# A hybrid attention / state-space / delta-rule layer: convolution and gate-row DMAs moved from SyncE's queue to GpSimd's

## The chip, the core and the metric

The kernel runs on one core of a Trainium2 chip. The metric is the time of one execution on the device in microseconds (us). The core has TensorE (PE in the profile, with its weight loads as PEld), VectorE (DVE), ScalarE (ACT), GpSimd (POOL) and SyncE (SP). Each engine works through its own list of instructions in order. SP computes nothing here: its list is a list of DMA issues. A DMA issue that has to wait for a buffer or for another transfer holds up everything behind it in the list of the same engine.

## The reference

One layer on 256 tokens of width 4096. The input is RMS-normalised and multiplied by one wide matrix of 14392 columns. Those columns feed three groups of heads: a forgetting-attention group, a Mamba-2 group (SSD) and a gated DeltaNet group. Then a product with `w_out` and the residual. The parts that the change touches are the causal depthwise convolution over four tokens, which the DeltaNet q, k, v and the SSD x, B, C pass, and the cumulative gates ("rows" of decays) that each group needs on all partitions.

```
h    = rms_norm(x, norm_w)
proj = einsum('bsd,de->bse', h, w_in)            # 14392 columns, split among the groups
xbc  = silu(causal_depthwise_conv(ssd_xbc, ssd_conv_w) + ssd_conv_b)
qkv  = silu(causal_depthwise_conv(gdn_qkv, gdn_conv_w))
y    = ssd_scan(xs, dt, A, B, C)                 # decays exp(cumsum) between tokens
o    = gated_delta_rule(gq, gk, gv, g, beta)     # chunked solve, decays exp(cumsum)
o_f  = fox_attention(q, k, v, log_f)             # softmax with cumulated forget gates
out  = x + einsum('bse,ed->bsd', concat(o_f, y, o), w_out)
```

## The kernel before

The projection is cut into 28 panels of 512 columns (`UNITS`), and `w_out` into 8 more. A panel has 32 steps of 128 input rows. In each step a 128x512 piece of float32 weight is split into a high part `wh` (ScalarE, L203) and a low part `wl` (VectorE, L204). Six matmuls of 128x128 by 128x512 follow: for each of two blocks of tokens one with `wh` and the high part of x (L214), one with `wh` and the low part (L215), and one with `wl` (L216). There are 1152 such steps and 6912 such matmuls. They are the bulk of the program, and everything else is laid between them. The gate columns have a small product of their own at the start.

Weights come in pieces of two steps (512 KB, tile `wr`, four buffers) issued on SP by `panel` (L226) and, for the first two panels, by `first_panels` (L280). `wh` and `wl` have five buffers each, so ScalarE and VectorE can run at most five steps ahead of TensorE.

At the end of a panel ScalarE copies the two results out of PSUM into a tile `raw_...` (L1002, three buffers) and starts that unit's own work: a Python generator whose pieces are put between the steps by `drive()`, one piece per step; `yield 6` skips six steps. There are two lists of generators, `prep` (convolution and the like, one unit after another) and `core` (the heads themselves).

For a unit with a convolution, `conv_unit` stores the raw tile into a DRAM buffer `past` (L454), which has three zero rows in front, and reads it back shifted by one, two and three tokens (`shift`, L467). The four rows of filter weights are read as broadcasts over the partitions (`tap`, L458). VectorE multiplies and adds (L471, L476, L477, L485). There are 14 such units: gq, gk, gv for three groups, sB, sC, and sx for three thirds. `shift` tiles have two buffers, so the third shifted load waits until the first one is used up; `tap` tiles have three.

`gate_rows` (L423) reads rows of cumulated gates from a small DRAM tensor `gsum` as broadcasts (`dmat`, `e0`, `em`), 26 times; `gates` writes it once (L415). `clear_past` (L446) writes the zero rows.

All of these DMAs are issued on SP, between the loads of the weights. GpSimd has 73 instructions in the profile: a few elementwise products per head (`ktail` L571, `dmat` L600, `ds` L601, `tt` L639, `res` L664, `xd` L798 and so on).

The order on each engine is not the order of the text alone. The program is put in order by a list scheduler of the tile framework, which keeps a model of when each engine and queue is free; `pin` keeps the marked instructions in the order of the text among themselves. So a DMA that is put on another engine also changes where its neighbours stand.

Of the kernel before, what the change touches and what calls it, by code (L numbers as in the profile page):

```python
# [19 lines left out]
P = 128  # L20
D = 4096
T = 256
# [11 lines left out]
NSP = NDT + NGA + NFF  # L34
# [20 lines left out]
CONV = {}  # L55
# [3 lines left out]
TAPS = 4  # L59
# [32 lines left out]
def tile_hybrid(ctx: ExitStack, tc: tile.TileContext, x, xT, w, wo, prm, cst, lev, cvw, out):  # L92
    nc = tc.nc
# [12 lines left out]
    def r4(shape, dt=F32, name="r4", tag="acc"):  # L106
        return hp.tile(shape, dt, tag=tag, name=name, bufs=BUFS[tag])

    def t2(shape, dt=F32, name="t2", tag="t2"):
        return hp.tile(shape, dt, tag=tag, name=name, bufs=BUFS[tag])  # L110
# [7 lines left out]
    def bank(name="bank"):  # L118
        return ph.tile([P, 512], F32, tag="bank", name=name)
# [7 lines left out]
    def mid(ap, n):  # L127
        return ap.unsqueeze(1).broadcast_to([P, n, ap.shape[1]])


    pin = tc.keep_in_program_order
# [217 lines left out]
    def gates():  # L349
        gr = raw["gates"]  # L350
        pre = t2([P, 2, NSP], name="pre")
        nc.vector.tensor_tensor(out=pre, in0=gr[:, :, 0:NSP], in1=mid(prm_s[:, C_BIAS:C_BIAS + NSP], 2), op=ALU.add)
        f0 = NDT + NGA
        nc.vector.tensor_scalar_mul(pre[:, :, f0:NSP], pre[:, :, f0:NSP], -1.0)
        pf = pre.rearrange("p a b -> p (a b)")
        n = 2 * NSP
        ab = t2([P, n], name="g_ab")
        nc.vector.scalar_tensor_tensor(out=ab, in0=pf, scalar=-1.0, in1=pf, op0=ALU.mult, op1=ALU.max)
        e = t2([P, n], name="g_e")
        nc.scalar.activation(e, ab, AF.Exp, scale=-1.0)  # L360
        be = cp.tile([P, 2, NBE], F32, name="be")
        nc.scalar.activation(be, gr[:, :, NSP:NG], AF.Exp, scale=-1.0)
        ea = t2([P, NSP], name="ea")
        nc.vector.memset(ea[:, f0:NSP], -1.0)
        nc.scalar.activation(ea[:, 0:f0], prm_s[:, C_ALOG:C_ALOG + f0], AF.Exp)
        nc.vector.tensor_scalar_mul(ea[:, 0:f0], ea[:, 0:f0], -1.0)
        yield 2

        u = t2([P, n], name="g_u")
        nc.vector.tensor_scalar_add(u, e, 1.0)  # L370
        res = t2([P, n], name="g_r")
        nc.vector.scalar_tensor_tensor(out=res, in0=u, scalar=-1.0, in1=e, op0=ALU.add, op1=ALU.subtract)
        ru = t2([P, n], name="g_ru")
        nc.vector.reciprocal(ru, u)
        nc.vector.tensor_tensor(out=res, in0=res, in1=ru, op=ALU.mult)
        lu = t2([P, n], name="g_lu")
        nc.scalar.activation(lu, u, AF.Ln)
        yield 2
        nc.vector.tensor_tensor(out=lu, in0=lu, in1=res, op=ALU.subtract)
        spl = cp.tile([P, 2, NSP], F32, name="spl")  # L380
        nc.vector.scalar_tensor_tensor(out=spl.rearrange("p a b -> p (a b)"), in0=pf, scalar=0.0, in1=lu,
                                       op0=ALU.max, op1=ALU.add)
        ga = cp.tile([P, 2, NSP], F32, name="ga")
        nc.vector.tensor_tensor(out=ga, in0=spl, in1=mid(ea, 2), op=ALU.mult)
        yield

        nc.vector.tensor_scalar_add(be, be, 1.0)
        nc.vector.reciprocal(be, be)
        nbe = cp.tile([P, 2, NBE], F32, name="nbe")
        nc.vector.tensor_scalar_mul(nbe, be, -1.0)  # L390

        yield 2
        ps = bank("gps")
        nc.tensor.matmul(ps[:, 0:f0], U, ga[:, 1, 0:f0], start=True, stop=True)
        nc.tensor.matmul(ps[:, f0:2 * f0], SL, ga[:, 0, 0:f0], start=True, stop=True)
        dec = cp.tile([P, 2, f0], F32, name="dec")
        nc.scalar.activation(dec.rearrange("p a b -> p (a b)"), ps[:, 0:2 * f0], AF.Exp)


        yield  # L400
        ps = bank("csps")
        for tb, m in ((0, SL), (1, U)):
            o = tb * NSP
            nc.tensor.matmul(ps[:, o:o + f0], st["mid_u"], ga[:, tb, 0:f0], start=True, stop=True)
            nc.tensor.matmul(ps[:, o + f0:o + NSP], m, ga[:, tb, f0:NSP], start=True, stop=True)
        cs = cp.tile([P, 2, NSP], F32, name="csum")
        nc.vector.tensor_copy(cs.rearrange("p a b -> p (a b)"), ps[:, 0:2 * NSP])
        nc.vector.tensor_scalar_mul(cs[:, 1, f0:NSP], cs[:, 1, f0:NSP], -1.0)
        yield
        ps = bank("csrow")  # L410
        for tb in range(2):
            nc.tensor.transpose(ps[0:NSP, tb * P:tb * P + P], cs[:, tb, :], ident)
        rows = t2([P, 2, P], name="csrows")
        nc.scalar.copy(rows[0:NSP, :, :], ps[0:NSP, 0:2 * P].rearrange("p (a b) -> p a b", a=2))
        nc.sync.dma_start(out=gsum.rearrange("t h l -> h t l"), in_=rows[0:NSP, :, :])  # L415
        st.update(spl=spl, cs=cs, be=be, nbe=nbe, gam=dec[:, 0, :], tail=dec[:, 1, :])

    gsum = dp.tile([2, NSP, P], F32, name="gsum")

    def gate_rows(tb, c0, n, name, tag="t2", into=None):  # L420

        t = t2([P, n, P], name=name, tag=tag) if into is None else into
        pin(nc.sync.dma_start(out=t.rearrange("p a b -> p (a b)"),  # L423
                              in_=gsum[tb:tb + 1, c0:c0 + n, :].rearrange("o h l -> o (h l)").broadcast_to([P, n * P])))
        return t

    def decay(t, tb, c0, n):
# [11 lines left out]
    past = dp.tile([len(CONV), TAPS - 1 + T, 512], F32, name="past")  # L439

    def clear_past(after):
        z = t2([P, 512], name="zrows")
        nc.vector.tensor_copy(z[:, 0:1], after)
        nc.vector.memset(z, 0.0)
        for r in range(TAPS - 1):
            nc.sync.dma_start(out=past[:, r, :], in_=z[0:len(CONV), :])  # L446

    def conv_unit(name, dst=None, bias=False):


        src = raw.pop(name)
        i = list(CONV).index(name)
        yield
        pin(nc.sync.dma_start(out=past[i, TAPS - 1:TAPS - 1 + T, :].rearrange("(b p) c -> p b c", b=2), in_=src))  # L454

        def taps(r):
            t = t2([P, 512], name="tap", tag="tap")
            pin(nc.sync.dma_start(out=t, in_=cvw[i, r:r + 1, :].broadcast_to([P, 512])))  # L458
            return mid(t, 2)

        tap = [taps(r) for r in range(TAPS - 1, 0, -1)]
        yield 6

        def shifted(j):
            sh = r4([P, 2, 512], name="shift")
            r = TAPS - 1 - j
            pin(nc.sync.dma_start(out=sh, in_=past[i, r:r + T, :].rearrange("(b p) c -> p b c", b=2)))  # L467
            return sh

        got = [shifted(j) for j in (1, 2)]  # L470
        pin(nc.vector.tensor_tensor(out=src, in0=src, in1=tap[0], op=ALU.mult))  # L471
        yield
        tap.append(taps(0))
        yield 5
        for j in range(1, TAPS):
            pin(nc.vector.tensor_tensor(out=got[j - 1], in0=got[j - 1], in1=tap[j], op=ALU.mult))  # L476
            pin(nc.vector.tensor_tensor(out=src, in0=src, in1=got[j - 1], op=ALU.add))  # L477
            yield 1
            if j == 1:
                got.append(shifted(3))  # L480
                if bias:
                    tap.append(taps(TAPS))
            yield 1 if j == 1 else 4 if j == 2 else 1
        if bias:
            nc.vector.tensor_tensor(out=src, in0=src, in1=tap[TAPS], op=ALU.add)  # L485
            yield
        nc.scalar.activation(src if dst is None else dst, src, AF.Silu)  # L487
        yield
        return src
# [96 lines left out]
    def gdn_solve(g):  # L586

        qk, m32, m16 = [], [], []
        dr = [gate_rows(tb, NDT + HG * g, HG, "dmat") for tb in range(2)]
        yield 6  # L590
        for tb in range(2):
# [198 lines left out]
    def ssd_group(g):  # L790
        hh = slice(6 * g, 6 * g + 6)
        y_off = None
        for tb in range(2):
            xd = t2([P, 6, 64], name="xd", tag="qk")
            for u, a, n, o in pieces(g):
# [3 lines left out]
                                        op=ALU.mult)  # L799
            m = []  # L800
            dr = [gate_rows(tb, 6 * g + 3 * i, 3, "dmat") for i in range(2)]
            yield 6
            for i in range(2):
# [179 lines left out]
    def fox_out(g, z):  # L983
        yield from gated_norm(fx[f"ot{g}"], fx[f"c{g}"], z)
        yield from to_mix(fx[f"ot{g}"], 24 + 4 * g, C_FO)

    HEAD = {"ga": lambda i: gates(), "gq": gdn_q, "gk": gdn_k, "gv": gdn_v, "gz": gdn_z, "sB": ssd_b, "sC": ssd_c,
            "sx": ssd_x, "sz": ssd_z, "fq": fox_q, "fk": fox_k, "fv": fox_v, "fz": fox_z}

# [39 lines left out]
    for i in range(8):  # L1029
        cs = slice(i * 512, (i + 1) * 512)  # L1030
        ps = panel(wo[i].rearrange("p (j n) -> p j n", n=512), mix_split)
        for tb in range(2):
# [3 lines left out]
            n = 2 if i == 7 and tb == 1 else 1  # L1036
            for q in range(n):
# [3 lines left out]
                                                        in_=xr[:, qs])  # L1041
# [51 lines left out]
```

## Time and profile before

| | |
|---|---|
| median of 3 executions | 1717.98 us (1716.26 to 1718.16) |
| the profiled execution | 1718.33 us |
| its span, first to last instruction | 1716.5 us |
| PE busy | 1709.2 us (100%) |
| PEld busy | 1410.8 us (82%) |
| DVE busy | 1173.9 us (68%) |
| ACT busy | 930.1 us (54%) |
| POOL busy | 97.3 us (6%) |
| DMA moved | 368.87 MB, mean 215 GB/s |

Times in the views count from the first instruction of the span. A matmul's busy time is longer than the distance from its start to the next one's start, since they are pipelined; so 100% busy does not say that TensorE could not be faster, but a gap in it is a gap. Issuing instructions of SP are not counted as busy.

### The profile page before, as it was taken

The numbers are of one execution on the slowest core, as the hardware profiler recorded it, in microseconds if no ns is written. First come the engines' busy times: TensorE is split into PE (matmuls) and PEld (weight loads), VectorE is DVE, ScalarE is ACT, GpSimd is POOL, SyncE is SP. The second block draws the span as 40 slices with busy tenths as digits, with TensorE's granted clock in tenths as the row PEclk, the third lists the DMA queues.
The fourth block names the chain that finished last, engine by engine and source line by source line (L and its number), as shares of the span: only waits on it lengthen the run. The fifth ranks groups of instructions, "written<-read, shape, count | busy, mean of one in ns | idle before, by whom it ended". The sixth has DMA issues, their size and how long they took to land.

```text
span 1716.5 us, 24082 instructions
## 1 busy us (share of the span) xinstructions
PE 1709.2 (100%) x8165; PEld 1410.8 (82%) x8165; DVE 1173.9 (68%) x2121; ACT 930.1 (54%) x1611; POOL 97.3 (6%) x73
## 2 busy tenths in 40 slices
PE   9999999999999999999999999999999999999999
PEld 7888888888888788888888888888888888888887
DVE  7767777878776976869876765555656665555554
ACT  6665555455445544545555665556555754444443
POOL 0000030002000120001221100000000000000000
PEclk9999999999999999999999999999999999999999
DMA  8778777665766757758886666665666577777774
GB/s 288 232 240 272 257 244 228 221 202 164 248 208 205 244 172 225 246 172 295 261 257 196 184 184 186 193 196 172 185 194 192 178 236 217 218 218 215 208 208 136
DMA packets 119508, 368.87 MB, mean 215 GB/s; under 512 B 12629, under 2 KB 16045, under 8 KB 119383
## 3 DMA queue, kind: packets, MB, share of 16 engines
q1 hardware_dynamic: 114055, 358.15, 67.3%
q10 hardware_dynamic: 5328, 9.17, 1.5%
q8 instruction: 64, 1.05, 0.2%
q14 instruction: 61, 0.50, 0.1%
HBM read 355.61 MB, written 11.67 MB: 214 GB/s over the span
## 4 chain that ended last, share of the span: by engine, by line
PE 99%; DVE 0%; ACT 0%; issue 0%; DVEq 0%; ACTq 0%
PE proj L216 31%; PE proj L214 30%; PE proj L215 30%; PE kkps L610 1%; PE yp L818 1%; PE zps L583 0%; PE yps L583 0%; PE zqs L583 0%; PE gproj L243 0%; PE mps L508 0%; PE cor L583 0%; PE o L583 0%; PE vn L583 0%; PE atps L583 0%; PE warmps L154 0%; PE fps L900 0%
## 5 line engine op out<-in xcount | busy, mean ns | idle before, releaser
L204 DVE TENSOR_TENSOR wl<-wr,wh 128x512 fp32r<-128x512 f32 x1152 | 804.2, 711 | 480.6 <-ACT wh L203 418.2
L203 ACT CAST wh<-wr 128x512 fp32r<-128x512 f32 x1152 | 707.8, 621 | 713.1 <-PE proj L215 335.2
L214 PE MATMUL proj<-wh,xhl 128*128 128x512 f32 x1792 | 706.8, 395 | 2.1 <-ACT raw_gz L1002 1.9
L215 PE MATMUL proj<-wh,xhl 128*128 128x512 f32 x1792 | 701.2, 391 | 0.0
L216 PE MATMUL proj<-wl,xhl 128*128 128x512 f32 x1792 | 682.7, 395 | 0.0
L214 PEld LDWEIGHTS proj<-wh,xhl 128*128 128x128 f32 x1792 | 337.1, 188 | 72.2 <-ACT raw_gz L1002 2.3
L215 PEld LDWEIGHTS proj<-wh,xhl 128*128 128x128 f32 x1792 | 337.0, 188 | 69.1
L216 PEld LDWEIGHTS proj<-wl,xhl 128*128 128x128 f32 x1792 | 335.2, 188 | 68.6 <-DVE wl L204 0.2
L215 PE MATMUL proj<-wh,mhl 128*128 128x512 f32 x512 | 199.2, 389 | 0.0
L214 PE MATMUL proj<-wh,mhl 128*128 128x512 f32 x512 | 199.1, 390 | 0.0
L216 PE MATMUL proj<-wl,mhl 128*128 128x512 f32 x512 | 195.2, 390 | 0.0
L215 PEld LDWEIGHTS proj<-wh,mhl 128*128 128x128 f32 x512 | 96.1, 188 | 20.1
L214 PEld LDWEIGHTS proj<-wh,mhl 128*128 128x128 f32 x512 | 96.1, 188 | 19.9
L216 PEld LDWEIGHTS proj<-wl,mhl 128*128 128x128 f32 x512 | 96.1, 188 | 19.9
L476 DVE TENSOR_TENSOR shift<-shift,tap 128x1024 f32<-128x1024 f32 x42 | 52.5, 1250 | 8.3 <-DMA shift<-past 8.3
L655 DVE TENSOR_TENSOR tn<-tn,zps 128x512 f16<-128x512 f16 (+1 forms) x36 | 24.5, 681 | 3.7 <-PE zps L583 3.7
L656 DVE TENSOR_TENSOR tt<-tt,zqs 128x512 f16<-128x512 f16 (+1 forms) x36 | 24.4, 679 | 0.0
L664 POOL TENSOR_TENSOR res<-cst_s,tn 128x512 f32<-128x512 f32 x6 | 7.8, 1304 | 252.5 <-DVE tn L655 162.9
L646 ACT CAST y<-yps 128x512 f16<-128x512 f32 x36 | 19.4, 585 | 2.7 <-PE yps L583 2.7
L798 POOL TENSOR_TENSOR xd<-xtok,spl 128x384 f32<-128x384 f32 (+2 forms) x12 | 11.8, 994 | 129.9 <-ACT xtok L487 65.7
L600 POOL TENSOR_TENSOR dmat<-dmat,cst_s 128x512 f32<-128x512 f32 x6 | 10.1, 1694 | 154.2 <-ACT dmat L436 154.2
L173 DVE SCALAR_TENSOR_TENSOR xhl<-xr,xhl 128x256 fp32r<-128x256 f32 x32 | 15.3, 478 | 3.4 <-ACT xhl L172 3.4
(301 smaller groups left out, 937.8 us busy)
## 6 DMA issues: line engine op xcount, KB each, us to landing
wr<-in_w SPq DMA_DIRECT2D x446, 512.0 KB, 3.8
wr<-in_wo SPq DMA_DIRECT2D x128, 512.0 KB, 3.6
shift<-past SPq DMA_DIRECT2D x42, 512.0 KB, 5.8
tap<-in_cvw SPq DMA_DIRECT2D x61, 256.0 KB, 5.2
xres<-in_x ACTq DMA_DIRECT2D x16, 256.0 KB, 4.9
xr<-in_xT SPq DMA_DIRECT2D x15, 257.0 KB, 5.2
out<-xres ACTq DMA_DIRECT2D x15, 256.0 KB, 4.1
dmat<-gsum SPq DMA_DIRECT2D x16, 192.0 KB, 5.1
```

Of the source, the lines that this page charges most:

```text
L173: pin(nc.vector.scalar_tensor_tensor(out=t[:, 1, :], in0=xr[:, jj, 0:T], scalar=sc, in1=t[:, 0, :].bitcast(F32), op0=ALU.mult, op1=ALU.sub ...
L203: a = nc.scalar.copy(wh, wr)
L204: b = nc.vector.tensor_tensor(out=wl, in0=wr, in1=wh.bitcast(F32), op=ALU.subtract)
L214: nc.tensor.matmul(ps[tb], h, wh, start=k == 0, stop=False)
L215: nc.tensor.matmul(ps[tb], lo, wh, start=False, stop=False)
L216: nc.tensor.matmul(ps[tb], h, wl, start=False, stop=k == KT - 1)
L476: pin(nc.vector.tensor_tensor(out=got[j - 1], in0=got[j - 1], in1=tap[j], op=ALU.mult))
L610: nc.tensor.matmul(ps[:, i * T:(i + 1) * T], kq[:, h, 0, :], kq[:, h, :, :], start=True, stop=True)
L646: nc.scalar.copy(y[tb], v4(ps))
L655: nc.vector.tensor_tensor(out=tn2, in0=tn[tb], in1=v4(zp), op=ALU.subtract)
L656: nc.vector.tensor_tensor(out=tt2, in0=tt[tb], in1=v4(zq), op=ALU.subtract)
L818: nc.tensor.matmul(yp[:, h * 64:h * 64 + 64], m[h // 3][:, h % 3, :], xd[:, h, :], start=True, stop=True)
```

## The change

Six `nc.sync.dma_start` become `nc.gpsimd.dma_start`: the store of the gate rows, their loads, the zero rows of `past`, the store of the raw tile, the loads of the taps and the shifted loads. Nothing else in the text of the kernel differs: buffers, `yield` numbers and arithmetic are the same.

```
-        nc.sync.dma_start(out=gsum.rearrange("t h l -> h t l"), in_=rows[0:NSP, :, :])
+        nc.gpsimd.dma_start(out=gsum.rearrange("t h l -> h t l"), in_=rows[0:NSP, :, :])
...
-        pin(nc.sync.dma_start(out=t.rearrange("p a b -> p (a b)"),
-                              in_=gsum[tb:tb + 1, c0:c0 + n, :].rearrange("o h l -> o (h l)").broadcast_to([P, n * P])))
+        pin(nc.gpsimd.dma_start(out=t.rearrange("p a b -> p (a b)"),
+                                in_=gsum[tb:tb + 1, c0:c0 + n, :].rearrange("o h l -> o (h l)").broadcast_to([P, n * P])))
...
-            nc.sync.dma_start(out=past[:, r, :], in_=z[0:len(CONV), :])
+            nc.gpsimd.dma_start(out=past[:, r, :], in_=z[0:len(CONV), :])
...
-        pin(nc.sync.dma_start(out=past[i, TAPS - 1:TAPS - 1 + T, :].rearrange("(b p) c -> p b c", b=2), in_=src))
+        pin(nc.gpsimd.dma_start(out=past[i, TAPS - 1:TAPS - 1 + T, :].rearrange("(b p) c -> p b c", b=2), in_=src))
...
-            pin(nc.sync.dma_start(out=t, in_=cvw[i, r:r + 1, :].broadcast_to([P, 512])))
+            pin(nc.gpsimd.dma_start(out=t, in_=cvw[i, r:r + 1, :].broadcast_to([P, 512])))
...
-            pin(nc.sync.dma_start(out=sh, in_=past[i, r:r + T, :].rearrange("(b p) c -> p b c", b=2)))
+            pin(nc.gpsimd.dma_start(out=sh, in_=past[i, r:r + T, :].rearrange("(b p) c -> p b c", b=2)))
```

The built program shows what this does to the order on the engines. First SP in the kernel before, from the store of the raw tile of gv of the third DeltaNet group (`gv_5742`) to the last shifted load of that unit; `wr` are the weights.

```order
L454 DMA past<-raw_gv_5742 128x2x512
L458 DMA tap<-in_cvw 128x512
L226 DMA wr<-in_w 128x1024 x2
L458 DMA tap<-in_cvw 128x512
L226 DMA wr<-in_w 128x1024 x4
L458 DMA tap<-in_cvw 128x512
L226 DMA wr<-in_w 128x1024
L467 DMA shift<-past 128x2x512
L226 DMA wr<-in_w 128x1024
L467 DMA shift<-past 128x2x512
L226 DMA wr<-in_w 128x1024
L458 DMA tap<-in_cvw 128x512
```

The last rows of SP in the changed kernel, from the end of the first two panels on:

```order
L237 DMA gwr<-in_w 128x448
L226 DMA wr<-in_w 128x1024 x414
L226 DMA wr<-in_wo 128x1024 x128
L1040 DMA out<-xres 128x256
L1080 UNCONDITIONAL_BRANCH
```

After the first two panels SP has nothing left but weights, and one piece of the output.

Now GpSimd at the same place, the third DeltaNet group. Before, from the correction `res` of the second group on:

```order
L664 TENSOR_TENSOR res<-cst_s,tn_4971 128x512
L664 TENSOR_TENSOR res<-cst_s,tn_5007 128x512
L600 TENSOR_TENSOR dmat<-dmat,cst_s 128x512
L601 TENSOR_TENSOR ds<-dmat,cst_s 128x512
L600 TENSOR_TENSOR dmat<-dmat,cst_s 128x512
L571 TENSOR_TENSOR ktail<-raw_gk_5249,dec 128x512
L601 TENSOR_TENSOR ds<-dmat,cst_s 128x512
L639 TENSOR_TENSOR tt<-idh,mb 128x512 x2
```

The same stretch in the changed kernel, from `ktail` on:

```order
L571 TENSOR_TENSOR ktail<-raw_gk_5249,dec 128x512
L454 DMA past<-raw_gv_5742 128x2x512
L458 DMA tap<-in_cvw 128x512 x3
L467 DMA shift<-past 128x2x512 x2
L458 DMA tap<-in_cvw 128x512
L467 DMA shift<-past 128x2x512
L423 DMA dmat<-gsum 128x512 x2
L600 TENSOR_TENSOR dmat<-dmat,cst_s 128x512
L601 TENSOR_TENSOR ds<-dmat,cst_s 128x512
L600 TENSOR_TENSOR dmat<-dmat,cst_s 128x512
L601 TENSOR_TENSOR ds<-dmat,cst_s 128x512
```

The convolution of gv now stands behind `ktail` of gk in GpSimd's list, and `ktail` reads the result of gk's convolution and normalisation. Before, the two convolutions were under way at the same time.

VectorE follows that. Before, around the end of gk's convolution (`raw_gk2_5249`) and the start of gv's (`raw_gv2_5742`):

```order
L476 TENSOR_TENSOR shift_5511<-shift_5511,tap_5419 128x1024
L204 TENSOR_TENSOR wl_6026<-wr_6012,wh_6025 128x512
L204 TENSOR_TENSOR wl_6038<-wr_6035,wh_6037 128x512
L477 TENSOR_TENSOR raw_gk2_5249<-raw_gk2_5249,shift_5511 128x1024
L476 TENSOR_TENSOR shift_5843<-shift_5843,tap_5773 128x1024
L204 TENSOR_TENSOR wl_6052<-wr_6035,wh_6051 128x512
L204 TENSOR_TENSOR wl_6064<-wr_6061,wh_6063 128x512
L477 TENSOR_TENSOR raw_gv2_5742<-raw_gv2_5742,shift_5843 128x1024
L204 TENSOR_TENSOR wl_6074<-wr_6061,wh_6073 128x512
L496 TENSOR_REDUCE ssqk_5080<-sq_5616 128x4
L496 TENSOR_REDUCE ssqk_5080<-sq_5631 128x4
L204 TENSOR_TENSOR wl_6086<-wr_6083,wh_6085 128x512
```

The same stretch in the changed kernel:

```order
L476 TENSOR_TENSOR shift_5511<-shift_5511,tap_5419 128x1024
L204 TENSOR_TENSOR wl_6052<-wr_6035,wh_6051 128x512
L477 TENSOR_TENSOR raw_gk2_5249<-raw_gk2_5249,shift_5511 128x1024
L204 TENSOR_TENSOR wl_6064<-wr_6061,wh_6063 128x512
L204 TENSOR_TENSOR wl_6074<-wr_6061,wh_6073 128x512
L204 TENSOR_TENSOR wl_6086<-wr_6083,wh_6085 128x512
L496 TENSOR_REDUCE ssqk_5080<-sq_5616 128x4
L496 TENSOR_REDUCE ssqk_5080<-sq_5631 128x4
L204 TENSOR_TENSOR wl_6096<-wr_6083,wh_6095 128x512
L559 TENSOR_SCALAR ssqk_5080<-ssqk_5080 128x16
```

Before, products of gv's convolution stand between gk's last sum and its norm. After, there are only splits of weights between them, and gv's convolution follows 13 splits after gk's last sum.

## Rows read from the trace of the kernel before

**Rows 1.** The page: span, busy time, and the chain that ended last.

```profile
span 1716.5 us, 24082 instructions
PE 1709.2 (100%) x8165; PEld 1410.8 (82%) x8165; DVE 1173.9 (68%) x2121; ACT 930.1 (54%) x1611; POOL 97.3 (6%) x73
...
PE 99%; DVE 0%; ACT 0%; issue 0%; DVEq 0%; ACTq 0%
```

**Rows 2.** All waits of PE after its start: who, for whom, us, times, longest.

```profile
PE proj L214 <- ACT raw_gz L1002: 1.9, 1, 1.9
...
PE proj L214 <- ACT wh L203: 0.3, 1, 0.3
```

**Rows 3.** Windows: us, busy PE, PEld, DVE, ACT, POOL, granted PE clock, DMA share, GB/s.

```profile
590.00:595.00 5.00, 4.75 (x21) 3.60 (x20) 5.00 (x15) 2.72 (x4) 0.00 (x0) 1.00 1.01 391
595.00:600.00 5.00, 3.13 (x13) 2.19 (x12) 5.00 (x7) 4.97 (x9) 4.50 (x2) 0.93 0.34 94
600.00:605.00 5.00, 5.00 (x18) 4.01 (x17) 5.00 (x8) 4.06 (x6) 4.16 (x2) 0.73 0.70 234
...
800.00:900.00 100.00, 100.00 (x463) 82.61 (x462) 84.01 (x131) 58.30 (x93) 24.33 (x25) 1.00 0.82 261
1400.00:1500.00 100.00, 100.00 (x442) 82.78 (x442) 53.02 (x81) 44.17 (x75) 0.00 (x0) 1.00 0.71 216
```

**Rows 4.** Timeline of SP, 574 to 599 us: start, us, engine, line, operation, tiles.

```profile
576.28 0.33 SPq L226 DMA_DIRECT2D wr<-in_w  x1
580.24 0.33 SPq L458 DMA_DIRECT2D tap<-in_cvw  x1
580.84 0.33 SPq L226 DMA_DIRECT2D wr<-in_w  x1
582.58 0.38 SPq L467 DMA_DIRECT2D shift<-past  x1
583.05 0.90 SPq L423 DMA_DIRECT2D dmat<-gsum  x2
```

**Rows 5.** Timeline of ACT and DVE, 575 to 600 us.

```profile
592.26 1.14 ACT L203 CAST wh<-wr 128x512 fp32r<-128x512 f32 x2 [4.36 <-DVE wl L204]
597.32 1.25 ACT L1002 ACTIVATE raw_gz<-proj,xn_y 128x512 f32<-128x512 f32 x2
...
578.98 1.23 DVE L476 TENSOR_TENSOR shift<-shift,tap 128x1024 f32<-128x1024 f32 x1 [2.13 <-DMA shift<-past]
595.79 1.25 DVE L309 TENSOR_SCALAR rsqk_t<-ssqk 128x16 int32<-128x16 int32 x1
```

**Rows 6.** DMA issues by line: tiles, queue, operation, count, KB each, us to landing.

```profile
shift<-past SPq DMA_DIRECT2D x42, 512.0 KB, 5.8
tap<-in_cvw SPq DMA_DIRECT2D x61, 256.0 KB, 5.2
dmat<-gsum SPq DMA_DIRECT2D x16, 192.0 KB, 5.1
```

**Rows 7.** The shifted loads: issue (ns min, median, max), landing, who waited.

```profile
L467 SPq DMA_DIRECT2D shift<-past x42: 371/377/1279, 110.5 to 869.8; - x42
...
  DMA shift<-past: 8.3, 6
...
DMA to landing us min/median/max: 3.6/5.8/9.2
```

**Rows 8.** GpSimd's two gate products over the run; the DVE operation L309 on `rsqk_t`.

```profile
L600 POOL TENSOR_TENSOR dmat<-dmat,cst_s x6: 1307/1670/2453, 236.5 to 601.7; 128x512 f32<-128x512 f32 x6
L601 POOL TENSOR_TENSOR ds<-dmat,cst_s x6: 1725/1789/4649, 239.4 to 612.4; 128x512 f32<-128x512 f32 x6
L309 DVE TENSOR_SCALAR rsqk_t<-ssqk x3: 166/167/1255, 181.6 to 595.8; 128x16 int32<-128x16 int32 x3
```

**Rows 9.** Timeline around two low points of VectorE's lead, 406 and 500 us.

```profile
406.21 0.68 DVE L204 TENSOR_TENSOR wl<-wr,wh 128x512 fp32r<-128x512 f32 x1
407.00 0.44 PE L216 MATMUL proj<-wl,xhl 128*128 128x512 f32 x1
...
500.23 1.89 DVE L204 TENSOR_TENSOR wl<-wr,wh 128x512 fp32r<-128x512 f32 x3
501.11 0.71 PE L216 MATMUL proj<-wl,xhl 128*128 128x512 f32 x2
```

**Rows 10.** Waits of ACT for weights over the whole run.

```profile
ACT wh L203 <- DMA wr<-in_w: 37.4, 17, 4.6
```

## The prediction

> **What bounds the kernel now.** I read the page first, then the waits of TensorE, then windows of time around those waits, then the timelines of SP, ScalarE and VectorE in them. On the page TensorE is busy 1709.2 of 1716.5 us, and the chain that ended last is 99% PE [rows 1]. A pipelined matmul is recorded as longer than its distance to the next, so I take the pace from a quiet stretch: in 1400 to 1500 us there are 442 matmuls in 100 us, 226 ns from one to the next [rows 3], so a step of six takes 1.36 us. The change takes no matmul away. What it can give back is time in which TensorE stood still or ran slowly. After its start TensorE waited twice, 0.3 and 1.9 us [rows 2], both in 590 to 600 us, where the busy time is 4.75 and 3.13 of 5 us: 0.25 + 1.87 = 2.1 us idle. After the longer gap the granted clock falls: the means are 0.93 and 0.73 in two windows of 5 us, that is a stay at 1.2 instead of 2.4 GHz [rows 3]. It costs 5 x 0.07 + 5 x 0.27 = 1.7 us. Together 3.8 us is all that a better feed of TensorE can return.
>
> **Where that stall comes from.** TensorE waited for ScalarE's copy of a finished panel out of PSUM (`raw_gz`, L1002), at 597.32 us. ScalarE was late: it had stood idle for 4.36 us before its piece of weight at 592.26 [rows 5]. The row names VectorE as releaser, but the weights are the likelier cause. On SP a tap load is issued at 580.24 and the next weight load only at 580.84, after 576.28; then come a shifted load, two gate rows and so on in the same list [rows 4]. In 590 to 595 the DMA engines are full, 1.01 at 391 GB/s [rows 3]. So weights stood behind convolution loads of two units at once, first as issues, then as transfers. VectorE was also behind, after waiting 2.13 us for a shifted load at 578.98 [rows 5].
>
> **The change part by part.**
>
> The SP list: 147 DMAs leave it: 42 shifted loads, 61 taps, 26 gate rows, 14 raw stores, 3 zero rows, 1 gate store; the three largest groups are in [rows 6]. SP keeps weights, which wait only for their own buffers. ScalarE waited 37.4 us for weights in 17 waits [rows 10]; most of that should go. It is worth almost nothing by itself, since TensorE's waits after the start sum to 2.2 us [rows 2]: the five buffers of split weights hid the rest. The order of the built program also pulls the convolutions of gk and gv of the third group apart, so the burst of transfers at 575 to 595 us, and the bunch of VectorE work in it, come one after the other. I take the stall as gone: -3.8 us. The bounds are -3.8 and 0.
>
> GpSimd's list: it has 97.3 us of work [rows 1] and gets 147 issues. The trace has no DMA issued by GpSimd. Bounds for an issue: 0.37 us, the median of a shifted load's issue on SP [rows 7], and 4.65 us, the longest of GpSimd's own `ds` products [rows 8]. At the upper end 147 x 4.65 = 684 us, and GpSimd is still idle for half of the span; so its total decides nothing. What counts is how late a load comes. I take 1.7 us, the median of GpSimd's `dmat` product [rows 8], the nearest plain row on that engine: 1.3 us later than SP.
>
> Most loads have room for it. In the changed order the first two shifted loads and the taps stand some ten steps or more ahead of their use in most units. The tight one is the third shifted load: its buffer comes free with the first sum and it is used 4 to 6 steps later in the changed order, 5.4 to 8.2 us. It lands 5.8 us after its issue in the median and 9.2 us at most [rows 7]. With 1.3 us more the median is 7.1 us: in about half of the 14 units VectorE waits about a microsecond longer. Behind a waiting product on VectorE stand the splits `wl`, and TensorE waits for those. VectorE waited 8.3 us in 6 waits for shifted loads before [rows 7] and TensorE felt next to nothing, since VectorE is up to five steps ahead. But its lead sinks low in the convolution stretch, where it is 84% busy against 53% later [rows 3]: at 406.89 us a split ends 0.1 us before its matmul, and near 500.9 the first of three ends 0.2 us before [rows 9]. I count two such places at 1.0 us each: +2.0 us. The bounds are 0 (a GpSimd issue as quick as SP's, or a load that is earlier for having no weight ahead of it; TensorE cannot gain from that beyond the stall) and 14 x (4.65 - 0.38) = 60 us.
>
> The Trainium skill (DMA: Bandwidth & Descriptors, Latency and other measured facts) gives about 1 us to the first byte for DMAs from GpSimd and 0.6 us from SP or ScalarE; by that estimate a load is 0.4 us later, the two places cost 0.8 us, and the sum would be 1715.0 us. No run here shows it yet.
>
> GpSimd computes in the same list. In the changed order `ktail` stands before the store of gv's raw tile, and gate products stand behind `dmat` loads that wait for a landing. Such waits move GpSimd's products by a transfer, some 5 us [rows 6]; TensorE's matmuls that need them were moved along in the order. I count nothing; the cover is the distance that the order leaves, and without it each costs up to 5 us, which is within the upper bound above.
>
> The zero rows, the gate store and the end of the program: the zero rows are written in the first two panels, long before the first shifted load, and the last product and store stay where they are. Nothing.
>
> Sum: 1718.33 (profiled execution: span 1716.5 and 1.8 around it) - 3.8 + 2.0 = 1716.5. The median of the runs shown, 1717.98, is 0.35 below the profiled one: forecast 1716.2 us. A difference under 0.2%, 3.4 us, counts as no change.
>
> **The rivals.**
>
> 1. The stall moves instead of going. Both orders have bunches of VectorE work at the convolutions of every group, and a panel's end somewhere near. For it: the low leads at 406 and 500 us, with no stall yet [rows 9]. Against: only one stall in 28 panels before. It keeps the 2.1 + 1.7 us: 1718 us. The words of the change speak of taps ten steps ahead, and nothing in its text moves a tap by a step; if the tap's buffers were the cause of the late weight at 580 us, they now hold up GpSimd instead, which has the same result as here or as in the forecast.
>
> 2. Slower: late third loads. An issue on GpSimd takes as long as its longest product, 4.65 us, because it stands behind a waiting neighbour or is held up by VectorE. Then each of the 14 third loads comes 4.3 us later; 2.4 us of that is covered where the distance is 6 steps (8.2 - 5.8). 1.9 us is left, 27 us in all if no lead is left, and 13 where it covers half. This decides from the point where the lateness passes the spare and the lead together, about 2 us in the tight units. For it: GpSimd's in-order list, VectorE's thin lead. Against: SP's issues are short, and GpSimd is idle 94% of the time [rows 1]. It gives 1718 - 3.8 + 13 = 1727 us.
>
> 3. Slower: VectorE itself is slowed. While GpSimd's `ds` took 4.65 us instead of 1.79, the small L309 on VectorE took 1.25 us instead of 0.17 [rows 8], at 595.79 us [rows 5]: the two block each other. If each of the 147 issues did that to VectorE, it would lose 147 x 1.08 = 159 us between about 100 and 960 us, 18 us in 100. It is 84% busy at its densest [rows 3], so it would be short by 2 us in 100 over some 400 us, 10 us, and more in bunches: 1718 - 3.8 + 15 = 1729 us. Against: an issue reads no tensor as `ds` does. The Trainium skill (SBUF — State Buffer, SBUF: two separate sides) warns of this pair: the port that they share is locked by one at a time, and descriptors of a GpSimd DMA cannot be written while VectorE runs an operation in a two-port mode. It would be the loads that are late, as in rival 2. The rows agree that the two engines block each other; none shows an issue.
>
> **How the numbers follow.** Forecast 0.48, its own range 1714 to 1718; rival 1 0.25; rival 2 0.19; rival 3 0.08. Without any new wait the forecast's case gives 1714.2, under the limit of 1714.5 for faster; with the 2.0 it is no change; I split it 0.25 and 0.23. Rival 1 is 0.02 faster, 0.20 the same, 0.03 slower; rival 2 is slower; rival 3 is 0.06 slower and 0.02 the same. Faster 0.27, same 0.45, slower 0.28. The range is 1712.5 to 1728: a little under the largest gain, for the spread of 2 us among the runs shown, and up to the middle of the two slower rivals, so that about 0.13 is left out above and 0.04 below.
>
> **What would show it.** Right: no gap of TensorE near 590 to 600 us and a clock of 1.00 there; SP waits for `wl` alone; ScalarE's waits for weights mostly gone; one or two short waits of TensorE in 400 to 850 us. The GpSimd term is wrong if a DMA row on GpSimd is far from 1.7 us or if shifted loads land much later than 7.1 us. Many waits of VectorE for `shift` with gaps of TensorE behind them would show rival 2, and longer `wl` at the times of GpSimd's issues rival 3. The whole is wrong if TensorE's gaps lie outside the convolution stretch.

## The result and the profile after

The changed kernel takes 1726.8 us (median of 4 runs, 1725.1 to 1727.75) against 1717.1 for the kernel before (1716.2 to 1718.2): a ratio of 1.0059, 95% interval 1.0046 to 1.0072. Forecast was no change, at 1716.2 us. The measured time lies inside the stated range, 1712.5 to 1728, only because that range reached up to two slower rivals. The profiled execution takes 1727.75 us.

The page of the changed kernel: span, busy time and the chain that ended last; to be held against [rows 1].

```profile
span 1725.9 us, 24150 instructions
...
PE 1712.9 (99%) x8165; PEld 1411.3 (82%) x8165; DVE 1169.3 (68%) x2121; ACT 933.4 (54%) x1613; POOL 180.3 (10%) x220
...
PE 93%; issue 2%; DMA 2%; DVE 1%; POOL 1%; ACT 0%; DVEq 0%; POOLq 0%; ACTq 0%
```

TensorE has the same 8165 matmuls, but its chain now runs over transfers and GpSimd too. All of its waits, in the order who, for whom, us, times, longest:

```profile
PE proj L216 <- DVE wl L204: 6.0, 6, 1.9
PE yp L818 <- DVE dmat L809: 1.3, 1, 1.3
PE warmps L154 <- DVE warm L151: 1.2, 1, 1.2
```

Before there was one place at 590 to 600 us [rows 2, 3]; now there are seven, 7.3 us in sum, at 150, 430, 626, 634, 814, 824 and 872 us. The windows (columns as in [rows 3]) show that the old place is healed, and that a clock fall now stands behind the gap at 824 us:

```profile
595.00:600.00 5.00, 5.00 (x23) 4.14 (x23) 4.60 (x10) 3.69 (x6) 1.87 (x2) 1.00 0.66 196
...
822.00:827.00 5.00, 3.69 (x21) 2.81 (x20) 4.38 (x12) 4.28 (x8) 0.00 (x0) 0.93 1.02 379
827.00:832.00 5.00, 5.00 (x17) 3.98 (x17) 4.25 (x7) 1.48 (x3) 3.77 (x4) 0.73 0.82 252
```

Counted in steps of six matmuls, TensorE is 0.8 us behind the old kernel after its first step, at 8 us, before any of the moved transfers goes out (the first, at 24.94 us, is a zero row). It loses 1.7 more at steps 80 to 112, gains 4.2 at 368 to 400 (the healed stall), loses 2.8 at 400 to 416, 3.2 at 512 to 528 and 3.4 at 528 to 560. The steps between swing by up to 2.5 us and sum to about 1 us. From step 560 TensorE stays 8.9 us behind to the end. Apart from the first 0.8 us nothing is lost outside the stretch of the convolutions.

VectorE's waits for transfers; before they were 8.3 us for `shift` [rows 7], 2.0 for `dmat` and 0.3 for taps:

```profile
DVE shift L476 <- DMA shift<-past: 23.2, 15, 3.9
DVE dmat L430 <- DMA dmat<-gsum: 8.5, 8, 3.1
DVE raw_sx L471 <- DMA tap<-in_cvw: 3.9, 1, 3.9
DVE raw_gv L471 <- DMA tap<-in_cvw: 2.8, 1, 2.8
DVE raw_gq L471 <- DMA tap<-in_cvw: 2.5, 2, 1.5
```

The DMA issues, as in [rows 6], and the shifted loads by themselves, as in [rows 7]:

```profile
shift<-past POOLq DMA_DIRECT2D x42, 512.0 KB, 7.2
tap<-in_cvw POOLq DMA_DIRECT2D x61, 256.0 KB, 6.7
dmat<-gsum POOLq DMA_DIRECT2D x16, 192.0 KB, 5.4
```

```profile
L467 POOL DMA_DIRECT2D shift<-past x42: 704/713/755, 134.3 to 879.8; - x42
...
DMA to landing us min/median/max: 4.3/7.2/12.4
```

An issue on GpSimd is short, 0.71 us for a shifted load, and the load lands 1.4 us later after its issue than before. The decisive lines are another view, GpSimd's timeline from 577 to 616 us (start, us, engine, line, operation, tiles, and in brackets the idle time before):

```profile
577.48 0.70 POOL L467 DMA_DIRECT2D shift<-past  x1 [47.35 <-DVE raw_gk L477]
598.13 1.39 POOL L571 TENSOR_TENSOR ktail<-raw_gk,dec 128x512 f32<-128x512 f32 x1 [19.95 <-DVE sqn L721]
599.47 0.76 POOL L454 DMA_DIRECT2D past<-raw_gv  x1
600.23 1.63 POOL L458 DMA_DIRECT2D tap<-in_cvw  x3
604.76 1.44 POOL L467 DMA_DIRECT2D shift<-past  x2 [2.90 <-DMA past<-raw_gv]
```

GpSimd stands for 19.95 us at its own product `ktail`, and the store of gv's raw tile, its taps and its shifted loads stand behind it in the list. VectorE waits for one of these taps at 606.87 us, and TensorE's next two gaps follow at 626 and 634 us (timelines of the two engines):

```profile
606.87 1.23 DVE L471 TENSOR_TENSOR raw_gv<-raw_gv,tap 128x1024 f32<-128x1024 f32 x1 [2.79 <-DMA tap<-in_cvw]
```

```profile
626.24 0.74 PE L216 MATMUL proj<-wl,xhl 128*128 128x512 f32 x2 [0.88 <-DVE wl L204]
...
633.66 0.50 PE L216 MATMUL proj<-wl,xhl 128*128 128x512 f32 x1 [1.17 <-DVE wl L204]
```

A like picture stands before the gap at 824 us: the product `xd` (L798) waits 9.99 us for ScalarE, the gate rows go out behind it at 815.38 us, and VectorE waits 3.15 us for them at 821.57. But this gap is not the queue's alone: with the same order and the transfers on SyncE, below, TensorE still waits 1.3 us for the same `dmat` (L809), at 817 us.

### The profile page after: what moved, and what is told of

It reads as the page before. It is cut to its first block, busy times and chain, and to the rows that moved or that the text cites. A ratio compares the mean times of both kernels' runs of the same rounds, so it can differ in the third digit from the quotient of the medians.

```text
span 1725.9 us, 24150 instructions
## 1 busy us (share of the span) xinstructions
PE 1712.9 (99%) x8165; PEld 1411.3 (82%) x8165; DVE 1169.3 (68%) x2121; ACT 933.4 (54%) x1613; POOL 180.3 (10%) x220
## 4 chain that ended last, share of the span: by engine, by line
PE 93%; issue 2%; DMA 2%; DVE 1%; POOL 1%; ACT 0%; DVEq 0%; POOLq 0%; ACTq 0%
PE proj L216 29%; PE proj L214 29%; PE proj L215 29%; DMA dmat<-gsum 1%; DMA tap<-in_cvw 1%; PE yp L818 1%; PE zps L583 0%; PE yps L583 0%; PE zqs L583 0%; PE gproj L243 0%; PE kkps L610 0%; PE cor L583 0%; DVE wl L204 0%; DMA shift<-past 0%; PE mps L508 0%
## 5 line engine op out<-in xcount | busy, mean ns | idle before, releaser
L467 POOL DMA_DIRECT2D shift<-past x42 | 30.2, 720 | 216.5 <-DVE raw_gk L477 71.6
L458 POOL DMA_DIRECT2D tap<-in_cvw x61 | 33.6, 554 | 146.3 <-DVE shift L476 37.5
L430 DVE TENSOR_SCALAR dmat<-dmat,csum 128x128 f32<-128x128 f32 x72 | 19.9, 338 | 8.5 <-DMA dmat<-gsum 8.5
L892 POOL TENSOR_TENSOR raw_fq<-raw_fq,frs_y 128x1024 f32<-128x1024 f32 x2 | 4.3, 2172 | 187.4 <-ACT wh L203 187.4
```

Of the source, the lines that this page charges most:

```text
L430: pin(nc.vector.tensor_scalar(out=t[:, i, :], in0=t[:, i, :], scalar1=st["cs"][:, tb, c0 + i:c0 + i + 1], scalar2=0.0, op0=ALU.subtract, o ...
L458: pin(nc.gpsimd.dma_start(out=t, in_=cvw[i, r:r + 1, :].broadcast_to([P, 512])))
L467: pin(nc.gpsimd.dma_start(out=sh, in_=past[i, r:r + T, :].rearrange("(b p) c -> p b c", b=2)))
```

## The experiments

Theory 1: GpSimd's queue brings the loads late, and VectorE waits. Theory 2: the loads matter little; the change gives all engines a new order, and that order has gaps. All ratios are to the kernel before on the same chip.

**One part at a time.** Each of these issues one part of the transfers by `nc.gpsimd` and leaves the rest on SyncE:

```
taps_only:   - pin(nc.sync.dma_start(out=t, in_=cvw...      + pin(nc.gpsimd.dma_start(out=t, in_=cvw...
shift_only:  the same in the raw store, the zero rows and shifted(j)
gates_only:  the same in the gate store and gate_rows
```

> Kernel before with the 61 tap loads alone on GpSimd's queue; stores, shifted loads and gate rows stay on SP. Theory 1 (late loads: what GpSimd issues lands about 1.4 us later than what SP issues, and VectorE, which takes its work in order, stands before the late load with the weight splits behind it): taps land at 6.7 us instead of 5.2, VectorE waits some 5 us for taps in all, TensorE gaps of 1 to 2 us, and the gap of before at 592 to 600 us goes if the tap wait on SP made it: 1714 to 1718 us. Theory 2 (the loads are not to blame: the new order of VectorE's and TensorE's work makes the gaps): a change of up to 3 us either way with no wait of VectorE for taps before the gaps.

> Kernel before with the raw stores, the zero rows and the 42 shifted loads alone on GpSimd's queue; taps and gate rows stay on SP. Theory 1: shifted loads land at about 7.2 us, VectorE waits about 20 us for them in 12 to 15 waits instead of 8.3 in 6, TensorE has three or four gaps of 0.5 to 1 us: 1717 to 1722 us, the larger share of the 9.7 us. Theory 2: gaps without a wait of VectorE for a shifted load ahead of them.

> Kernel before with the store and the 26 loads of gate rows alone on GpSimd's queue; the convolution's DMAs stay on SP. Theory 1: gate rows land little later (5.4 against 5.1 us), but stand behind waiting products in GpSimd's list; VectorE waits up to 8 us for them; one gap of TensorE near 820 us as in the changed kernel (1.3 us and the clock's 1.7): 1717 to 1720 us. Theory 2: no wait for gate rows ahead of a gap.

Measured: taps 1722.5 us, 1.0034 (1.0022 to 1.0046); stores and shifted loads 1721.3, 1.0027 (1.0016 to 1.0037); gate rows 1717.0, 1.0004 (0.9996 to 1.0013). By the medians that is 6.3, 5.2 and 0.8 us. Shifted loads went as theory 1 had it: VectorE waits 26.0 us for them in 13 waits, and TensorE's gaps for `wl` sum to 5.2 us; the twelve executions spread widely, from 1717.2 to 1727.4 us. Gate rows make VectorE wait 11.9 us, and TensorE has no gap near 820 us. Most of the loss of the taps, as the profiled execution shows it, is not one that the change has. Alone on GpSimd and with no store ahead of them, the first three taps go out at the very start, among the first loads of x and weights:

```profile
1.25 1.77 POOL L458 DMA_DIRECT2D tap<-in_cvw  x3 [0.80 <-POOLq L1089]
```

ScalarE then waits 2.15 us for a weight at 8.62 us, TensorE stands still for 1.15 and 0.50 us at 9.3 and 11.0 us, and the granted clock falls to a mean of 0.66 in 10 to 15 us. TensorE is 3.4 us behind the old kernel by step 6, at 17 us, of 4.2 in the whole profiled execution. In the changed kernel the first tap leaves at 128.78 us, behind the first raw store. Each kernel also has its own order and its gaps elsewhere (taps: also 406 and 612 us; shifted loads: 405, 787 and 806 us), so the three can't be added.

**More distance.** The pauses in a convolution unit made longer, first in the changed kernel, then, as a control, in the kernel before:

```
-        yield 6                                          +        yield 9
-            yield 1 if j == 1 else 4 if j == 2 else 1    +            yield 1 if j == 1 else 7 if j == 2 else 1
```

> Changed kernel with three more steps between a convolution's loads and its first product (yield 6 to 9) and three more before the third shifted product (yield 4 to 7). Theory 1: VectorE's waits for shift and tap fall below 12 us in all and TensorE's gaps below 3 us: 1717 to 1721 us. Theory 2: the gaps stay near 7 us, since the amount and the order of VectorE's work stay: 1725 to 1728 us.

> The kernel before with the two longer pauses of a convolution unit (6 to 9, and 4 to 7 before the third product); every transfer stays on SyncE. It is the control to the same edit in the changed kernel, which left that at 1727.4 us. Theory 1: without GpSimd's queue the new pauses cost little, 1714 to 1719 us, and VectorE's waits for shifted loads fall below the 8.3 us of before. Theory 2: another order and other gaps, as much as with GpSimd's queue: 1720 to 1727 us with waits of VectorE for loads under 10 us.

Measured: 1727.4 us, 1.0064 (1.0051 to 1.0077), and 1728.1, 1.0074 (1.0062 to 1.0086). The first looked like evidence against theory 1. It is none: VectorE still waits 32 us for transfers in it, so the longer pauses did not bring the distance that they were meant to bring. The control shows besides that the pauses cost 12.7 us with all transfers on SyncE, where VectorE waits only 4.2 us for shifted loads. So an edit of the order can cost as much as the change. In the control's trace TensorE waits 4.4 us for `wl` and 3.0 us, at 824 us, for GpSimd's product `xd`, and its clock falls behind that wait (mean 0.50 in 825 to 830 us); why `xd` and the splits are late there is open.

**A fourth tap buffer, and the gate store back on SyncE.**

```
before_tap4, after_tap4:  "tap": 3  ->  "tap": 4    (graw and ga moved to other buffers)
after_gsum_sp:            - nc.gpsimd.dma_start(out=gsum...    + nc.sync.dma_start(out=gsum...
```

> The kernel before with four tap buffers instead of three (two small gate tiles share other buffers to make room); every transfer stays on SyncE. Theory 1 (the loads that GpSimd issues land late, and VectorE waits for them): nothing is late here, and if the wait for a tap buffer in SyncE's list was what held the weights back at 576 to 581 us, the stall at 590 to 600 us goes: 1712.5 to 1715 us, waits of VectorE for shifted loads about 8 us as before. Theory 2 (each order of VectorE's and TensorE's work has its own gaps, because VectorE's lead is thin, whatever issues the loads): the order is another one, so the gaps of TensorE stand elsewhere: 1714 to 1724 us.

> The changed kernel with four tap buffers instead of three. Theory 1: GpSimd's list waits less for tap buffers, so loads behind a tap come earlier; VectorE's waits for taps (9.2 us) and shifted loads (23.2 us) fall to about 25 us together and the time to 1720 to 1725 us. Theory 2: another order, gaps elsewhere, 1720 to 1728 us with no tie to the waits for loads.

> The changed kernel with the one store of the gate sums back on SyncE. Behind that store, which waits 100.7 us for ScalarE's rows, stood the first convolution unit's store and loads in GpSimd's list. Theory 1: the first unit's loads come some 24 us earlier, the 1.8 us that TensorE lost there and the first gap at 150 us go, the rest stays: 1724 to 1726 us. Theory 2: another order, 1720 to 1728 us, with gaps elsewhere and the loss there not tied to the store.

Measured: 1716.2 us, 1.0001 (0.9992 to 1.0009); 1725.7, 1.0056 (1.0042 to 1.0070); 1726.2, 1.0059 (1.0047 to 1.0071). The first missed theory 1's number: its longest gap of TensorE is 0.5 us and its profiled execution 2.9 us shorter than that of before, but the medians are the same. The profiled execution of before took 1718.3 us, the median beside this run is 1715.5, and of the 77 executions of the kernel before beside the experiments 58 took less than 1717 us; so perhaps not every execution has the stall at its full size. No trace of those executions was kept. In the second, VectorE's waits for taps and shifted loads fall from 32.4 to 23.5 us, as theory 1 had it, but those for gate rows rise from 8.5 to 14.4, and the time hardly moves: the tap buffers are not what makes the loss. With the gate store on SyncE the 1.7 us at steps 80 to 112 are gone, as theory 1 had it, but steps 544 to 560 now lose 4.6 us against the kernel before, where the changed kernel loses 2.1.

**The same order, two queues.** Every kernel so far was ordered anew. These keep the order in which the program is written (the built program's reordering is switched off). The instructions then stand nearly alike with either queue: the traces of the first two have the same order on TensorE, and instructions a few places apart have changed places at 26 of 2121 positions on VectorE, 9 of 1608 on ScalarE and 6 of GpSimd's 73 products:

```
-    with tile.TileContext(nc, schedule_with_timeline_sim=True) as tc:
+    with tile.TileContext(nc, schedule_with_timeline_sim=False) as tc:
```

> The kernel before, with its instructions left in the order in which the program writes them (no reordering of the built program). It is the base of a pair: in this order the instructions of TensorE, VectorE, ScalarE and GpSimd's compute stand word for word alike whether the convolution's loads are issued by SyncE or by GpSimd. Both theories: slower than the reordered kernel, 1720 to 1900 us, since a wait now stands where it is written.

> The changed kernel in the written order: against its pair only the queue that issues the 147 transfers differs, no compute instruction is moved. Theory 1 (loads land later by GpSimd's queue, VectorE waits, TensorE behind it): slower than its pair by 4 to 15 us, with VectorE's waits for shifted loads, taps and gate rows up by 20 us or more. Theory 2 (only the order of VectorE's and TensorE's work made the loss): within 3 us of its pair, or faster by what SyncE's list gave back.

> The changed kernel in the written order, with the one gate store back on SyncE. In the written pair the loss of the changed queue came at one place: +6.7 us in steps 96 to 112, where the first unit's store and loads stand behind the gate store in GpSimd's list and go out at 119.7 us where SyncE sent them at 105.6 us. If that store is the cause, those 6.7 us go and the rest stays: 1729 to 1731 us, below the 1732.7 us of the written order with SyncE's queue. If the later landing of GpSimd's loads is the cause there, the loss stays: 1735 to 1737 us.

Measured: 1732.7 us, 1736.4 and 1738.8; the queue costs 3.7 us in the written order, a little less than theory 1 had forecast and a little more than theory 2. By steps the loss is one place, +6.7 us at 96 to 112; the rest sums to a gain of 2.8. There the gate store waits in GpSimd's list for ScalarE, and the first unit's transfers, sent at 105.6 us by SyncE, leave behind it (GpSimd's timeline in the changed kernel in written order, and TensorE's gap):

```profile
118.97 0.72 POOL L415 DMA_DIRECT2D gsum<-csrows  x1 [92.83 <-ACT csrows L414]
119.69 0.75 POOL L454 DMA_DIRECT2D past<-raw_gq  x1
120.43 1.65 POOL L458 DMA_DIRECT2D tap<-in_cvw  x3
```

```profile
152.75 0.80 PE L214 MATMUL proj<-wh,xhl 128*128 128x512 f32 x1 [3.73 <-ACT raw_gv L1002]
```

The third run missed its forecast. With the store on SyncE the first unit's store, taps and first shifted loads leave between 106.9 and 112.3 us, and the loss at steps 96 to 112 shrinks from 6.7 to 2.0 us, as it should if the store was in their way. But 3.7 us are now lost at steps 64 to 80. There ScalarE waits for a weight, and TensorE has two gaps of 1.7 us, at 119.9 and 121.9 us:

```profile
118.35 0.62 ACT L203 CAST wh<-wr 128x512 fp32r<-128x512 f32 x1 [4.98 <-DMA wr<-in_w]
```

The gate store is not what holds that weight up, for it is issued only at 122.59 us. In 115 to 120 us the DMA engines are full (share 1.02, 404 GB/s), with the first unit's transfers just issued beside the weights. So the transfers that leave earlier are the likelier cause of the late weight; that they are the whole of the 3.7 us was not shown.

**The order of the change, without its queue.** A table of the changed kernel's order pins TensorE, VectorE, ScalarE and GpSimd's products, instruction by instruction; the transfers are issued by SyncE, as before:

```
         tile_hybrid(tc, **args)
+        _chain(nc, tc)    # each instruction ordered behind the one that the changed kernel has before it
```

> Only the order of the change, without its queue: every transfer is issued by SyncE as before, and a table pins the instructions of TensorE, VectorE, ScalarE and GpSimd's compute into the order that the changed kernel has, instruction for instruction. Theory 1 (late loads by GpSimd's queue make the loss): most of the 10 us is gone, 1714 to 1719 us, and VectorE's waits for loads fall from 41 to about 15 us. Theory 2 (the new order makes the loss, whatever issues the loads): 1723 to 1729 us, with TensorE's gaps at the steps where the changed kernel has them.

Measured: 1717.9 us, 1.0013 (1.0004 to 1.0022). The traces of this kernel and the changed one have the same instructions in the same order on all four engines. Of the 9.7 us of the change about 1.8 go with the order (0.7 to 3.8 by the interval of its ratio) and 7.9 with the queue. The profiled execution, whose span is 1715.0 against 1725.9 us, was the fastest of eleven; two of the others took 1722 us. TensorE's and VectorE's waits in it:

```profile
PE yp L818 <- DVE dmat L809: 1.3, 1, 1.3
...
PE proj L216 <- DVE wl L204: 0.9, 2, 0.5
```

```profile
DVE shift L476 <- DMA shift<-past: 3.9, 3, 1.9
DVE dmat L430 <- DMA dmat<-gsum: 2.0, 3, 0.9
DVE raw_sx L471 <- DMA tap<-in_cvw: 1.5, 1, 1.5
```

That settles it for theory 1 in this order. Three of the seven places are left, at 426, 628 and 817 us, 2.2 us in sum. In this kernel gv's raw store is issued at 549.50 us, where the changed kernel issues it at 599.47. The next shifted load in SyncE's list is still gk's third:

```profile
549.50 0.38 SPq L454 DMA_DIRECT2D past<-raw_gv  x1
...
573.74 0.38 SPq L467 DMA_DIRECT2D shift<-past  x1
```

In the text gk's third load stands before gv's store, so on SyncE `pin` did not keep the order of the text. On GpSimd it did: in the changed kernel every unit's raw store comes behind the third shifted load of the unit before. At this place GpSimd stands 47.35 us before that load, until VectorE has used up its buffer (first line of GpSimd's timeline above). The change put the transfers behind one another's waits as well as behind the products.

**The queue of the change, without its place behind the products.** Theory 1 still has two causes: every load is issued and flies longer (1a), or the transfers stand behind GpSimd's own products (1b). In the next kernel the order is pinned as above, GpSimd issues the transfers, and each tap, store, shifted load and gate row is tied only to the one before it, no longer to the products (or the gate store) that the program has before it:

```
-    pin(nc.gpsimd.dma_start(...))     # behind all that the program has on GpSimd so far
+    pinq(nc.gpsimd.dma_start(...))    # behind the transfer before it
```

> The order of the change on TensorE, VectorE, ScalarE and among GpSimd's products is pinned as in the run before, but here GpSimd issues the transfers as in the change, and they are tied only to one another, no longer behind GpSimd's own products that stand before them in the program. Of the 9 us that the queue costs in this order: if its products in front of the transfers cost them (theory 1b: stores and loads stand behind a product that waits for another engine), most of it goes, 1717 to 1720 us, with VectorE's waits for loads under 25 us; if it is the longer flight of each load (theory 1a: issue 0.7 against 0.4 us and a landing about 1 us later), it stays, 1723 to 1728 us.

> The changed kernel with its transfers tied only to one another in GpSimd's list, and nothing pinned by a table, so the program is ordered anew. Theory 1b: 1713 to 1719 us, if the new order has no long gap of its own. Theory 1a: 1722 to 1728 us.

Measured: 1719.0 us, 1.0014 (1.0005 to 1.0023), and without the pinned order 1723.8, 1.0043 (1.0030 to 1.0055). GpSimd's timeline at the place shown above (lines are 8 further down in this kernel: L579 is the `ktail` product, L462 the raw store, L475 a shifted load):

```profile
575.05 0.70 POOL L475 DMA_DIRECT2D shift<-past  x1 [49.10 <-DVE raw_gk L485]
575.75 0.73 POOL L462 DMA_DIRECT2D past<-raw_gv  x1
576.48 1.11 POOL L466 DMA_DIRECT2D tap<-in_cvw  x2
583.32 0.54 POOL L466 DMA_DIRECT2D tap<-in_cvw  x1 [5.73 <-DVE shift L484]
584.69 1.44 POOL L475 DMA_DIRECT2D shift<-past  x2 [0.83 <-DMA past<-raw_gv]
597.83 1.39 POOL L579 TENSOR_TENSOR ktail<-raw_gk,dec 128x512 f32<-128x512 f32 x1 [11.70 <-DVE sqn L729]
```

The product stays where it was, and the store goes out 24 us earlier; it still leaves 26 us later than by SyncE, since it stands behind gk's third shifted load. The order of all products and matmuls is again that of the changed kernel. TensorE's waits for `wl` fall from 6.0 to 2.0 us and VectorE's for loads from 41 to 21. Against the changed kernel TensorE gains 1.4 us at steps 96 to 112 (where the first unit no longer stands behind the gate store), 2.2 at 400 to 416, 2.4 at 512 to 528 and 1.5 at 544 to 560: 7.5 of 8.1 us in the four places. And it does so with loads that fly no shorter:

```profile
shift<-past POOLq DMA_DIRECT2D x42, 512.0 KB, 8.4
tap<-in_cvw POOLq DMA_DIRECT2D x61, 256.0 KB, 6.7
```

So, by the medians over before, 6.8 us (9.7 - 2.9) belong to the place in GpSimd's list, behind the products and the gate store, and 1.8 to the order. What is left, 1.1 us (2.9 - 1.8), would be the longer issue and flight and the waits of the transfers behind one another; it is not told from nothing, since the ratios of the two pinned kernels are 1.0014 and 1.0013. The sizes hold for this order: in the written one the whole queue cost 3.7 us. The last kernel was ordered anew and came out in the range of theory 1a: VectorE again waits 21.5 us for shifted loads, and more than half of the gain is gone. Why this order does so is open; by itself it is no evidence for 1b, which rests on the pinned kernel. None of the fourteen kernels is faster than the one before.

## Why the prediction was wrong, point by point

**The stall at 590 to 600 us goes: right, but not the whole of a gain.** 4.2 us come back at steps 368 to 400, 3.8 were forecast. But the fourth tap buffer takes the same stall away (0.3 us are left of it) and is no faster by the median: what a single profiled execution shows as a stall was not to be had in full. And ScalarE's waits for weights, most of which were to go, only fell from 37.4 us to 27.2, in 19 waits.

**GpSimd's issue at 1.7 us: wrong; the landing: right by accident.** An issue takes 0.71 us for a shifted load and 0.55 for a tap; the flight made up for it, so that the median landing is 7.2 us, 7.1 forecast. By an estimate from the first-byte times in the Trainium skill (DMA: Bandwidth & Descriptors, Latency and other measured facts) a load would be 0.4 us later. Here the shifted loads landed 1.4 us later after their issue.

**Two places at 1.0 us: too few.** They were seven, 7.3 us, and one fall of the clock to 1.2 GHz, which costs about as much as the one that went (windows above: 0.35 and 1.35 us, 1.7 together).

**The step that failed** is the one on GpSimd's list: "GpSimd computes in the same list... Such waits move GpSimd's products by a transfer... I count nothing; the cover is the distance that the order leaves." It weighed how late a product comes behind a load, and not how late loads come behind a product. I had even named the pair, `ktail` before the store of gv's raw tile. In the trace after, GpSimd stands 19.95 us before `ktail`, with that store next in its list; the chain behind it is store, taps, shifted loads, products of VectorE, splits, matmuls. Taking the place behind the products away gives 6.8 of the 9.7 us back (order_after_free). The direction that was weighed cost VectorE one wait in the trace after, for `ds`, 1.20 us at 631.22. With it fell the sentence that the taps and the first two shifted loads have room: the first two shifted loads and the taps of gv left at 600 to 606 us for a first use at 606.87.

**The rivals.** Rival 2 gave the time, 1727 us, and half of the mechanism: a transfer that "stands behind a waiting neighbour". Its place was wrong (whole units and gate rows, not the third loads), and so was its price, the length of a product, where a wait for another engine is longer. That its sum came out at the measured time is luck. Its chance of 0.19 was too small: the order of the list showed the neighbour. Rival 3 is out: `wl` takes 710 ns in the mean, 711 before, and an issue never over 0.76 us. Rival 1 had the old stall come back at its old size; it is gone, and what came is another wait, for VectorE's split and not for ScalarE's copy.

## What to carry to other kernels

When transfers move to another engine's queue, read that engine's list as one line: for each transfer, the instruction ahead of it, what that waits for, and for how long. An engine that is idle 90% of its time can still be the worst place for a load, if it is idle because it waits. And before an order is blamed for a loss, pin it and change the queue alone; in a kernel whose lead falls to tenths of a microsecond, an edit can bring a new order that is worth as much as the edit. And when one part of a change is run alone, look where in time its loss lies before it is counted: the taps lost theirs at a place where the change has no tap.

## What the runs showed that I had not expected

- A transfer issued by GpSimd takes the engine 0.55 us (256 KB taps) to 0.71 us (512 KB shifted loads), SyncE 0.46 and 0.38 (medians); with the same order of compute the shifted loads land 8.4 us after their issue by GpSimd's queue and 6.4 by SyncE's.
- In one pinned order the 147 transfers make the kernel 1719.0 us by GpSimd's queue and 1717.9 by SyncE's, once they do not stand behind products: 2.0 us more to the landing of a shifted load cost about 1 us by the medians, which the intervals do not tell from nothing.
- Longer pauses between a load and its use cost 12.7 us with SyncE's queue (1728.1 us), although VectorE waited 4.2 us for shifted loads where it had waited 8.3.
